# Both products of the attention scores over 128 partitions: the low parts of the keys kept twice

## The chip, the core and the metric

The kernel runs as one launch on one core of a Trainium2 chip. The metric is the device time of that launch in microseconds (us). A difference between two kernels is read from repeated runs of both.

## The reference, cut to what matters

Two blocks follow each other, on 1024 tokens of 1024 channels, in float32. The first block holds a gated branch and an attention with 16 heads of 64 channels; the second a state-space layer, an embedding, an attention with 16 heads of 64 channels again ("stick-breaking"), and another embedding. The change concerns the scores of the two attentions alone, the products of queries with keys:

```python
# first block, dilated_pattern
s = jnp.einsum('bhrnqd,bhrnkd->bhrnqk', qb, kw) * (Dh ** -0.5)
...
# second block, stick_breaking_mixer, for each block of 128 queries
z = jnp.einsum('bhtd,bhsd->bhts', q[:, :, q0:kend], k[:, :, :kend]).astype(jnp.float32)
```

The kernel computes the first block's three dilated patterns as one causal attention over all earlier keys, with a table that is added to the scores. So both attentions have the same shape: for each head, eight tiles of 128 queries, each against all keys up to its own end.

## The kernel before, in words

Products run on TensorE (PE) in a rounded float32 type. To keep precision, an operand is held as a high part (the rounded value) and a low part (the rest), and a product is a sum of products of parts.

**Order.** A planner written in Python gives out the instructions: streams (generators) yield what they wait for, and the ready stream with the best priority goes on, judged by rough costs of each instruction. So the order in which each engine's instructions stand is fixed when the program is built, and a changed dependency or an added instruction changes that order from there on. On the chip each engine runs its list in order and waits on semaphores.

**Attention.** `attention1` (first block) and `stick` (second block) both work through eight pairs of heads. For a pair, `project_pair` makes four dense products (values, queries, keys, a gate), each 2 halves of 512 tokens times 24 matmuls of 128 rows and 512 columns. Between these, the streams of the scores, of the transposes of the weights and of the products with the values put in their own matmuls.

**Stacks.** The 64 channels of a head fill half of the 128 partitions, so `stacks_q` puts the high part of a head's queries on its own half and the low part on the other half. `stacks_k` writes the high part of the keys on both halves (ACT, four copies for each half of the tokens) and the low parts of both heads of the pair into one third tile, each on its own half (DVE, two subtractions, `lo_part`). The pools are cut in `stack_pools`: the tiles named m108r hold queries and high parts of the keys, m140r the low parts.

**Scores.** `scores` makes one tile of 128 queries against up to 512 keys with two matmuls that add into one bank of PSUM: the first contracts all 128 partitions (high and low queries against the high keys), the second contracts the 64 partitions of the head (high queries against the low keys). A head needs 12 such pairs of matmuls: 2 of 128 columns, 2 of 256, 2 of 384 and 6 of 512. For 16 heads and 2 attentions that makes 384 pairs.

**After the scores.** In `attention1` DVE adds the table and takes the maximum, ACT exponentiates, DVE normalises. In `stick` DVE adds a mask, ACT takes two sigmoids, DVE runs a scan (L2017) and POOL a multiplication. Then, in both, PE transposes the weights (L527), ACT and DVE split them (m156r), PE multiplies them with the values into a single bank of PSUM (`pv`), and ACT and DVE take the sum out (m192f).

Of the kernel before, what the change touches and what calls it, by code (L numbers as in the profile page):

```python
# [28 lines left out]
KB4 = 1024  # float32 elements in 4 KB  # L29
# [7 lines left out]
def at(scale, part):  # L37
    """a factor, or the part of a column of factors"""
    return scale if isinstance(scale, float) else scale[part, :]


class Tok:
    """estimated time at which something is ready; None until it is issued"""
# [5 lines left out]
class Bank:  # L49
    """a slot of PSUM"""  # L50
# [12 lines left out]
class Block:  # L63
    """a part of the arena that holds values of one kind at a time: "f" float32, "r" rounded for float32r products"""
# [5 lines left out]
class Arena:  # L70
    """storage of 4-byte values; off and n are in KB a partition"""

    CUTS = (0, 8, 16, 24, 40, 44, 60, 76, 92, 108, 140, 156, 172, 192, 200)
# [41 lines left out]
class Region:  # L115
    """a part of the arena; free when no overlapping region is held"""
# [25 lines left out]
class Ring:  # L142
    """storage given out in turn, sizes in KB"""
# [4 lines left out]
    def next(self, n):  # L148
        """region to be waited for and taken by the caller, in the order of the calls"""
        if self.pos + n > self.n:  # L150
            self.pos = 0
        r = self.b.region(self.off + self.pos, n)
        self.pos += n
        return r


class Res:
    """slots of storage, any of which will do"""
# [24 lines left out]
class Some:  # L183
    """n slots at once"""
# [10 lines left out]
class At(float):  # L195
    """time at which an engine is done with something"""
# [12 lines left out]
def seen(t, eng):  # L209
    """when engine eng can act on what is done at t"""  # L210
    own = getattr(t, "eng", None)
    return float(t) if own is None else t + (OWN[eng] if own == eng else LAT)
# [20 lines left out]
class Idle:  # L233
    """an engine without work given out ahead"""
# [9 lines left out]
class Sched:  # L244
    """Order of issue. Streams (generators) give instructions out and yield what their next ones wait for; the ready
    stream of the best priority goes on, judged by rough costs of the instructions given out so far."""
# [43 lines left out]
    def pe(self, ns, rows=P):  # L290
        """the clock of the tensor engine is halved in the tick after one with too little work"""
# [11 lines left out]
class Act:  # L303
    """activations, channels on partitions, split: quadrants [kh][th] of [128, 2 (hi, lo), 4 channel tiles, 512 tokens]"""
# [17 lines left out]
    def part(self, j, kh, t):  # L322
        """[128, 4, 128]: channel tiles of half kh, token tile t"""
        return self.quad(kh, t // 4)[:, j, :, (t % 4) * P:(t % 4) * P + P]

    def row(self, j, k, th):
        """[128, 512]: channel tile k, token half th"""
# [10 lines left out]
class Job:  # L338
    """one product; its weights are read in blocks [(granule, ...), ...] in the order of use"""

    def __init__(self, b, w, c0, ncols, kind, kt=KT, k0=0, gain=None, more=None):
        """more = (c, n): n columns from c on go with the last block"""
# [16 lines left out]
class Weights:  # L359
    """float32 blocks of up to 1024 values a partition, read ahead and split in the order in which they were added"""  # L360
# [53 lines left out]
    def limit(self, n, m=2):  # L414
        """use the first n split blocks and m unsplit ones only"""
# [6 lines left out]
class Builder:  # L422
# [28 lines left out]
    def banks(self, *names):  # L451
        """the banks to be used from now on for products, transposes, the rest of a phase, and sums"""
# [3 lines left out]
    def at(self, off, n):  # L456
        """n KB at off KB of the arena"""
        return self.arena.at(off, n)
# [72 lines left out]
    def evacuate(self, bank, r):  # L531
        """r: the time of the last read of the bank, or a stream that ends with it"""
# [9 lines left out]
    def gemm_b(self, act, job, evac, begin=None, each=None, free=None):  # L542
        """out[c, t] = sum_k w[k, c] x[t, k]; evac(cb, half, psum [128, 512], time) gives the time of its last read;
        free(half) when nothing reads that half of act any more"""
# [9 lines left out]
    def half_b(self, act, job, cb, half, evac, each):  # L554
        """gemm_b's product of one block and one half of the tokens"""
# [14 lines left out]
    def freed(self, act):  # L570
        """tokens of the times from which on nothing reads a half of act, and the function that sets them"""
# [9 lines left out]
    def gemm_a(self, act, job, evac, fin=None, k0=0, begin=None, late=()):  # L581
        """out[t, c]; evac(cb, tile, psum [128, 256], time), after begin(cb, tile); in the first block the tiles in late have banks of their own
        in which they wait for the last channels together"""
# [49 lines left out]
    def rstd(self, src, n, junk, dep, eps=EPS):  # L633
        """(mean of squares + eps) ** -0.5 of each row; stream"""
# [10 lines left out]
    def to_act(self, act, src, t, dep):  # L645
        """transposes of token tile t ([128 tokens, channels]) into act; stream"""
# [19 lines left out]
    def raw_tile(self, act, src, t, dep, nj, half):  # L666
        """act's token tile t = src, transposed; half[t] = half the factor of its norm; stream"""
# [12 lines left out]
    def norm_tile(self, act, src, t, g, dep, nj, done=None):  # L680
        """act's token tile t = rmsnorm(src) * g, transposed; stream"""
# [13 lines left out]
    def bcast(self, dst, row):  # L695
        """row [1, n] on every partition"""
        return self.dma(dst, row.to_broadcast([P, row.shape[1]]))

    def load_cols(self):
        """columns of channels in self.col; filled by the stream given back"""  # L700
# [36 lines left out]
    def plan(self):  # L737
        """products in the order in which they run, so that their weights can be read ahead"""
# [52 lines left out]
    def main(self):  # L791
        """the products, in order; everything else runs beside them"""
# [21 lines left out]
    def norm_in(self):  # L814
# [16 lines left out]
        def tile_(t):  # L831
            # the weights' first blocks come after the first tile
# [11 lines left out]
    def branch_a(self):  # L844
# [14 lines left out]
        def prep():  # L859
            # needed by the mixing only  # L860
# [75 lines left out]
    def spill(self, slots, kind, dst, toks, c0=0):  # L936
        """evac and each of channel-major products that go to DRAM; kind "silu2": 2 silu(x), "sig": tanh(x / 2) = 2 sigmoid(x) - 1"""
# [25 lines left out]
    def taken(self, region, blocks=0):  # L963
        """token of the time at which the region has become ours"""
# [12 lines left out]
    def load_act(self, act, rows, slots, mul=None, go=None):  # L977
        """streams: act's channel tiles from DRAM rows [(source, token)]; with mul: half the product with it"""
# [33 lines left out]
    def gates_a(self):  # L1012
        self.banks("01", "23", "456", "7")
        """silu of the attention gate to DRAM"""
# [6 lines left out]
    def merge(self):  # L1021
        self.banks("012", "3", "456", "7")
        """gate a * (ya @ w_proj_a) + gate b * (yb @ w_proj_b), split in act2; its product with w_out, two norms"""
# [4 lines left out]
        # the last gate fills the tail of the attention  # L1028
# [79 lines left out]
    def gated(self, act, job, gate, gtok, gl, out, dst, dtok):  # L1108
        """(gate + 1) * product to DRAM"""
# [27 lines left out]
    UNITS = [(h, g) for h in range(2) for g in (0, 1, 3, 2)]  # L1137

    def stack_pools(self):
        self.qsr, self.khr = self.res(108, 4, 4, "r"), self.res(124, 4, 4, "r")  # L1140
        self.klr, self.vsr = self.res(140, 4, 2, "r"), self.res(148, 8, 2, "r")

    def stacks_q(self, st, half, src, scale, e):
        """st = (head 0, head 1): own half of the partitions the high part, the other half the low part; stream"""
# [15 lines left out]
    def stacks_k(self, st, half, src, scale, e):  # L1160
        """st = (high parts of head 0 twice, of head 1 twice, low parts of both); stream"""
# [6 lines left out]
        for h, (own, oth) in enumerate(HALVES):  # L1168
            yield (e, s.FV)
            e = self.lo_part(st[2][own, tk], src[own, :], at(scale, own), st[h][own, tk], e)  # L1170
        return e

    def v_tile(self, vT, half, vs, e, done):
        """token-major stacks (high | low and low | high columns) of a pair from vT [128, 512]; stream"""
# [1065 lines left out]
```

## Time and profile before

| | before |
|---|---|
| median of 3 runs | 3373.07 us (3372.86 to 3374.96) |
| span of the profiled execution | 3370.6 us |
| instructions in it | 47748 |
| PE busy | 3229.0 us (96%) |
| DVE busy | 1680.2 us (50%) |
| ACT busy | 1364.6 us (40%) |
| POOL busy | 1257.3 us (37%) |

The span runs from the first to the last instruction of one profiled execution; some 2.5 us of the median lie outside it. Times in views are us from the start of the span, if not marked ns. Matmuls are pipelined: a row's duration runs to the modelled end of the matmul, and the next one can start before it. What a matmul costs its engine is therefore read as the distance from its start to the start of the next. "64\*128 64x512" means weights of 64 rows by 128 columns, and 64 rows by 512 columns that stream past them.

### The profile page before, as it was taken

The numbers are of one execution on the slowest core, as the hardware profiler recorded it, in microseconds if no ns is written. First come the engines' busy times: TensorE is split into PE (matmuls) and PEld (weight loads), VectorE is DVE, ScalarE is ACT, GpSimd is POOL, SyncE is SP. The second block draws the span as 40 slices with busy tenths as digits, with TensorE's granted clock in tenths as the row PEclk, the third lists the DMA queues.
The fourth block names the chain that finished last, engine by engine and source line by source line (L and its number), as shares of the span: only waits on it lengthen the run. The fifth ranks groups of instructions, "written<-read, shape, count | busy, mean of one in ns | idle before, by whom it ended". The sixth has DMA issues, their size and how long they took to land.

```text
span 3370.6 us, 47748 instructions
## 1 busy us (share of the span) xinstructions
PE 3229.0 (96%) x18830; PEld 2743.8 (81%) x18830; DVE 1680.2 (50%) x3080; ACT 1364.6 (40%) x2505; POOL 1257.3 (37%) x772
## 2 busy tenths in 40 slices
PE   8999999999999999988989889999999999998999
PEld 8888877777778889976868788899977777776899
DVE  2111156666664321556565564443457667677552
ACT  4322245545554311433232323213456556665421
POOL 3332111111112433234444444543335455557760
PEclk9999999999999999999999989999999999998999
DMA  4122211111112843323333334451201111112531
GB/s 133 51 76 78 78 62 58 52 51 51 57 55 85 274 157 137 102 72 73 107 79 105 80 107 124 144 198 38 82 22 38 38 37 35 36 38 93 189 118 51
DMA packets 296053, 291.35 MB, mean 86 GB/s; under 512 B 15556, under 2 KB 252276, under 8 KB 295828
## 3 DMA queue, kind: packets, MB, share of 16 engines
q1 hardware_dynamic: 295828, 288.29, 27.4%
q8 instruction: 148, 2.42, 0.3%
q14 instruction: 77, 0.63, 0.1%
HBM read 216.80 MB, written 71.43 MB: 86 GB/s over the span
## 4 chain that ended last, share of the span: by engine, by line
PE 82%; DVE 7%; DMA 6%; issue 2%; POOL 2%; ACT 1%; SPq 0%; POOLq 0%; ACTq 0%; DVEq 0%
PE psum L516 75%; PE psum L527 6%; DMA m92f<-acum 3%; DVE m24f L2017 2%; DMA m172f<-acum 1%; DVE m76f L493 1%; POOL m172f L501 1%; DVE m92f L489 1%; DVE m156r L482 1%; DVE m60f L493 0%; DMA m172f<-zd 0%; DVE m192f L482 0%; DVE m44f L493 0%; DMA m172f<-yd 0%; DVE m108r L493 0%
## 5 line engine op out<-in xcount | busy, mean ns | idle before, releaser
L501 POOL TENSOR_TENSOR m8r<-m0f,m8r 128x1024 fp32r<-128x1024 f32 (+1 forms) x67 | 169.4, 2529 | 538.1 <-ACT m8r L478 516.9
L501 POOL TENSOR_TENSOR m16r<-m0f,m16r 128x1024 fp32r<-128x1024 f32 x64 | 158.8, 2481 | 411.9 <-ACT m16r L478 406.4
L482 DVE TENSOR_TENSOR m156r<-psum,m156r 128x384 fp32r<-128x384 f32 (+2 forms) x376 | 221.6, 605 | 126.2 <-ACT m156r L478 125.0
L478 ACT ACTIVATE m156r<-psum 128x384 fp32r<-128x384 f32 (+2 forms) x376 | 194.0, 532 | 202.7 <-PE psum L527 196.4
L501 POOL TENSOR_TENSOR m24r<-m0f,m24r 128x1024 fp32r<-128x1024 f32 (+1 forms) x67 | 163.0, 2437 | 266.7 <-ACT m24r L478 263.6
L501 POOL TENSOR_TENSOR m172f<-m172f,m24f 128x127 f32<-128x127 f32 (+7 forms) x128 | 180.1, 1416 | 179.1 <-DVE m24f L2017 126.0
L2017 DVE TENSOR_TENSOR_SCAN m24f<-m24f,zero 128x128 f32<-128x128 f32 (+7 forms) x128 | 230.7, 1812 | 10.2 <-ACT m24f L478 9.5
L478 ACT ACTIVATE m192f<-psum 64x256 f32<-64x256 f32 (+2 forms) x240 | 105.0, 437 | 273.2 <-PE psum L516 194.8
L527 PE MATMUL psum<-ident,m172f 128*128 128x128 f32 (+1 forms) x1314 | 202.7, 278 | 10.7 <-POOL m172f L501 4.3
L493 DVE SCALAR_TENSOR_TENSOR m172f<-m172f,psum 128x256 f32<-128x256 f32 (+1 forms) x112 | 59.9, 534 | 279.8 <-ACT m172f L478 216.4
L516 PE MATMUL psum<-m140r,m108r 64*128 64x512 f32 (+3 forms) x384 | 170.7, 445 | 1.0 <-DVE m140r L493 1.0
L527 PEld LDWEIGHTS psum<-ident,m172f 128*128 128x128 f32 (+1 forms) x1314 | 149.5, 142 | 24.8 <-POOL m172f L501 5.2
L501 POOL TENSOR_TENSOR smalls<-smalls,mhalf 128x1 f32<-128x1 f32 (+1 forms) x104 | 83.4, 805 | 212.2 <-DVE smalls L489 202.5
L1410 ACT ACTIVATE m172f<-m172f,smalls 128x128 f32<-128x128 f32 (+7 forms) x128 | 99.1, 775 | 151.6 <-DVE smalls L489 151.5
L516 PE MATMUL psum<-m108r 128*128 128x512 f32 (+3 forms) x384 | 151.4, 394 | 3.9 <-ACT m172f L478 3.4
L1402 DVE CUSTOM_DVE_ANT_0 m172f<-psum,m24f 128x512 f32<-128x512 f32 (+1 forms) x192 | 106.6, 556 | 84.1 <-PE psum L516 81.0
L516 PEld LDWEIGHTS psum<-m140r,m108r 64*128 64x128 f32 x384 | 71.0, 185 | 93.7 <-issue 85.2
L501 POOL TENSOR_TENSOR m0f<-m0f,cols 128x1024 f32<-128x1024 f32 x64 | 129.1, 2018 | 27.8 <-PE psum L516 10.0
L478 ACT ACTIVATE m40f<-psum 128x256 f32<-128x256 f32 (+1 forms) x149 | 65.7, 444 | 177.7 <-PE psum L516 136.0
L516 PE MATMUL psum<-m60r,m8r 128*128 128x512 f32 x492 | 132.6, 402 | 0.0
L516 PE MATMUL psum<-m44r,m8r 128*128 128x512 f32 x492 | 131.7, 403 | 0.2 <-DVE m108r L493 0.2
L516 PE MATMUL psum<-m92r,m16r 128*128 128x512 f32 x480 | 131.0, 406 | 0.0
(361 smaller groups left out, 7991.9 us busy)
## 6 DMA issues: line engine op xcount, KB each, us to landing
m0f<-in_w_in_dram SPq DMA_DIRECT2D x72, 512.0 KB, 3.6
m0f<-in_m_in_dram SPq DMA_DIRECT2D x38, 512.0 KB, 4.5
m92f<-acum SPq DMA_DIRECT2D x21, 512.0 KB, 8.6
m24f<-in_alibi_dram SPq DMA_DIRECT2D x16, 512.0 KB
zd<-m40f SPq DMA_DIRECT2D x64, 128.0 KB, 1.9
m172f<-zd SPq DMA_DIRECT2D x32, 256.0 KB, 9.0
yd<-m172f SPq DMA_DIRECT2D x32, 256.0 KB, 2.2
m0f<-in_m_out_dram SPq DMA_DIRECT2D x16, 512.0 KB, 3.8
```

What stands on the lines that cost most here:

```text
L478: self.nc.scalar.activation(out, in_, func, **k)
L482: self.nc.vector.tensor_tensor(out, a, b, op=op)
L489: self.nc.vector.tensor_scalar(out, a, s1, s2, op0=op0, op1=op1)
L493: self.nc.vector.scalar_tensor_tensor(out, a, s, b, op0=op0, op1=op1)
L501: self.nc.gpsimd.tensor_tensor(out, a, b, op=op)
L516: self.nc.tensor.matmul(out, l, r, start=start, stop=stop)
L527: self.nc.tensor.transpose(out, in_, self.ident[:in_.shape[0], :in_.shape[0]])
L1402: nc.vector.tensor_tensor_reduce(row[:, k0:k0 + w], bank[:, :w], Tt[:, off + k0:off + k0 + w], 1.0, -3e38, op0=ALU.add, op1=ALU.max, accum ...
L1410: nc.scalar.activation(row[:, :n], row[:, :n], AF.Exp, bias=nm, accum_out=l)
L2017: nc.vector.tensor_tensor_scan(x[:, ::-1], x[:, ::-1], self.zero.to_broadcast([P, n]), 1.0, op0=ALU.mult, op1=ALU.add)
```

## The change

The low parts of each head's keys get a tile of their own, with the low part on both halves of the partitions. `stacks_k` writes the low part on the head's own half as before (DVE) and then ACT copies it to the other half. The second matmul of `scores` contracts all 128 partitions, so that it now also adds low queries times low keys. There are four tiles of low parts in place of two, the new ones in a new block of 16 KB at 200 KB (named m200r), and the builder is asked for a smaller area of DMA descriptors, which makes room for it. The changed file has no comments and docstrings either.

```diff
-    CUTS = (0, 8, 16, 24, 40, 44, 60, 76, 92, 108, 140, 156, 172, 192, 200)
+    CUTS = (0, 8, 16, 24, 40, 44, 60, 76, 92, 108, 140, 156, 172, 192, 200, 216)
...
-        self.klr, self.vsr = self.res(140, 4, 2, "r"), self.res(148, 8, 2, "r")
+        self.klr = Res([self.region(o, 4, "r") for o in (140, 144, 200, 204)])
+        self.vsr = self.res(148, 8, 2, "r")
...
         for h, (own, oth) in enumerate(HALVES):
             yield (e, s.FV)
-            e = self.lo_part(st[2][own, tk], src[own, :], at(scale, own), st[h][own, tk], e)
-        return e
+            lo = self.lo_part(st[2 + h][own, tk], src[own, :], at(scale, own), st[h][own, tk], e)
+            yield (lo, s.FA)
+            e2 = self.A(R(st[2 + h][oth, tk]), st[2 + h][own, tk], AF.Copy, lo)
+        return max(lo, e2)
...
-            yield from into("k", self.khr, self.khr, self.klr)
+            yield from into("k", self.khr, self.khr, self.klr, self.klr)
...
-        for x, r in zip(o["q"] + o["k"], (self.qsr, self.qsr, self.khr, self.khr, self.klr)):
+        for x, r in zip(o["q"] + o["k"], (self.qsr, self.qsr, self.khr, self.khr, self.klr, self.klr)):
...
     def scores(self, ps, o, h, i, k0, w):
-        own = HALVES[h][0]
         tk = slice(i * P, i * P + P)
         self.mm(ps, R(o["q"][h][:, tk]), R(o["k"][h][:, k0:k0 + w]), True, False)
-        return self.mm(ps, R(o["q"][h][own, tk]), R(o["k"][2][own, k0:k0 + w]), False, True)
+        return self.mm(ps, R(o["q"][h][:, tk]), R(o["k"][2 + h][:, k0:k0 + w]), False, True)
...
-    nc = _bacc.Bacc("TRN2", target_bir_lowering=False, num_devices=1)
+    nc = _bacc.Bacc("TRN2", dynamic_dma_scratch_size=1024, target_bir_lowering=False, num_devices=1)
```

The program has the same instructions on PE, DVE, POOL and the DMA queue as before, and 64 more on ACT. Their order differs from the first scores on. On PE, where `attention1` starts the scores of its first pair of heads, before the change (a row's shape is that of the result, so that the rows of the contraction don't show; m140r marks the second product; m92r and m44r are the dense product):

```order
L516 MATMUL psum<-m92r,m8r 128x512 x9
L516 MATMUL psum<-m108r 128x128
L516 MATMUL psum<-m140r,m108r 128x128
L516 MATMUL psum<-m108r 128x256
L516 MATMUL psum<-m140r,m108r 128x256
L516 MATMUL psum<-m92r,m8r 128x512 x3
L516 MATMUL psum<-m108r 128x384
L516 MATMUL psum<-m140r,m108r 128x384
```

The same place after the change:

```order
L516 MATMUL psum<-m92r,m8r 128x512 x12
L516 MATMUL psum<-m108r 128x128
L516 MATMUL psum<-m200r,m108r 128x128
L516 MATMUL psum<-m108r 128x256
L516 MATMUL psum<-m200r,m108r 128x256
L516 MATMUL psum<-m44r,m16r 128x512 x3
L516 MATMUL psum<-m108r 128x384
L516 MATMUL psum<-m200r,m108r 128x384
```

The two products stand in the same alternation; the second reads the new tile, and the scores moved behind three more matmuls of the dense product.

On ACT, where the same pair's stacks are made, before the change (m108r rows write queries and high keys, m24r, m16r and m8r rows are splits of weights, L1410 is the exponential):

```order
L478 ACTIVATE m108r<-psum 64x512 x4
L1410 ACT_TABLE_LOAD
L1410 ACTIVATE m172f,smalls<-m172f,smalls 128x128
L1410 ACTIVATE m172f,smalls<-m172f,smalls 128x256
L478 ACTIVATE m8r<-m0f 128x1024
L478 ACTIVATE m108r<-psum 64x512
```

The same place after the change (the exponential is L1412 there):

```order
L478 ACTIVATE m108r<-psum 64x512 x4
L478 ACTIVATE m200r<-m200r 64x512 x2
L478 ACTIVATE m8r<-m0f 128x1024
L478 ACTIVATE m108r<-psum 64x512
L1412 ACT_TABLE_LOAD
L1412 ACTIVATE m172f,smalls<-m172f,smalls 128x128
```

The two copies stand behind the high parts, and ahead of a split of weights and of the first exponential.

On ACT in `stick`, a pair of heads in the middle of the stage after the change (before, no row of m200r stood there; m24f and m172f are the two sigmoids, m40f a projection on its way out):

```order
L478 ACTIVATE m108r<-psum,smalls 64x512
L478 ACTIVATE m200r<-m200r 64x512
L478 ACTIVATE m40f<-psum 128x512
L478 ACTIVATE m200r<-m200r 64x512
L478 ACTIVATE m108r<-psum,smalls 64x512
L478 ACTIVATE m24f<-psum,rq 128x128
```

Each copy stands in the middle of ACT's list and waits there for its subtraction on DVE.

## Rows read from the trace of the kernel before

**Rows 1.** Page: span, then the chain that ended last, by engine.

```profile
span 3370.6 us, 47748 instructions
PE 82%; DVE 7%; DMA 6%; issue 2%; POOL 2%; ACT 1%; SPq 0%; POOLq 0%; ACTq 0%; DVEq 0%
```

**Rows 2.** Windows, by stage: most of attention1, most of stick, the state-space layer.

```profile
core 0: us, PE busy (x) PEld busy (x) DVE busy (x) ACT busy (x) POOL busy (x), PEclk, DMA share, GB/s
435.00:1080.00 645.00, 644.78 (x3206) 495.86 (x3205) 395.45 (x1076) 325.67 (x662) 79.31 (x33) 1.00 0.18 54
2480.00:3170.00 690.00, 652.99 (x3339) 503.80 (x3337) 494.27 (x680) 435.34 (x837) 406.61 (x243) 0.98 0.16 48
1400.00:2250.00 850.00, 765.02 (x4772) 677.65 (x4771) 459.81 (x763) 263.29 (x456) 374.24 (x248) 0.94 0.38 109
```

**Rows 3.** Timeline, PE, in attention1: start, length, engine, line, operation.

```profile
511.18 2.90 PE L516 MATMUL psum<-m60r,m8r 128*128 128x512 f32 x12
513.92 2.20 PE L516 MATMUL psum<-m92r,m8r 128*128 128x512 f32 x9
515.96 0.22 PE L516 MATMUL psum<-m108r 128*128 128x128 f32 x1
516.11 0.33 PE L516 MATMUL psum<-m140r,m108r 64*128 64x128 f32 x1
516.36 0.38 PE L516 MATMUL psum<-m108r 128*128 128x256 f32 x1
516.68 0.38 PE L516 MATMUL psum<-m140r,m108r 64*128 64x256 f32 x1
516.99 0.96 PE L516 MATMUL psum<-m92r,m8r 128*128 128x512 f32 x3
517.79 0.34 PE L516 MATMUL psum<-m108r 128*128 128x384 f32 x1
518.05 0.44 PE L516 MATMUL psum<-m140r,m108r 64*128 64x384 f32 x1
518.42 0.50 PE L516 MATMUL psum<-m108r 128*128 128x512 f32 x1
518.85 0.49 PE L516 MATMUL psum<-m140r,m108r 64*128 64x512 f32 x1
519.27 0.96 PE L516 MATMUL psum<-m44r,m16r 128*128 128x512 f32 x3
```

**Rows 4.** Timeline, weight loads (PEld) at the same place; idle in brackets.

```profile
513.69 2.00 PEld L516 LDWEIGHTS psum<-m92r,m8r 128*128 128x128 f32 x9
515.73 0.19 PEld L516 LDWEIGHTS psum<-m108r 128*128 128x128 f32 x1
516.11 0.18 PEld L516 LDWEIGHTS psum<-m140r,m108r 64*128 64x128 f32 x1 [0.18 <-issue]
518.85 0.18 PEld L516 LDWEIGHTS psum<-m140r,m108r 64*128 64x128 f32 x1 [0.24 <-issue]
```

**Rows 5.** Windows of m108r on PE (all score matmuls): attention1, stick.

```profile
435.00:1080.00 645.00, 139.73 (x384) 1.00 0.18 54
2480.00:3170.00 690.00, 147.47 (x384) 0.98 0.16 48
```

**Rows 6.** Lines by shape: ACT and DVE rows of the stacks, attention1 then stick.

```profile
L478 ACT ACTIVATE m108r<-psum 64x512 fp32r<-64x512 f32 x92 | 54.3, 590 | 12.0 <-PE psum L516 10.7
...
L2017 DVE TENSOR_TENSOR_SCAN m24f<-m24f,zero 128x1024 f32<-128x1024 f32 x16 | 42.8, 2677 | 0.0
...
L493 DVE SCALAR_TENSOR_TENSOR m140r<-psum,smalls,m108r 64x512 fp32r<-64x512 f32 x32 | 23.9, 747 | 6.4 <-ACT m108r L478 5.9
...
L478 ACT ACTIVATE m108r<-psum,smalls 64x512 fp32r<-64x512 f32 x96 | 65.4, 681 | 23.6 <-PE psum L527 22.1
```

**Rows 7.** Waits of PE in stick, 2400 to 3170: total, times, longest.

```profile
PE psum L516 <- DVE m156r L482: 16.3, 11, 4.5
PE psum L516 <- DVE m192f L482: 8.0, 7, 1.8
```

## The prediction, made before the changed kernel ran

> **What bounds the kernel now.** I read the chain that ended last first: PE makes 82% of it [rows 1]. The question is then how far each attention stage hangs on PE, so the windows by stage come next [rows 2]. In attention1 PE is busy 644.78 of 645 us, with DVE at 61%, ACT at 50% and POOL at 12%; the granted clock is 1.00, its upper level (2.4 GHz). This stage is as long as PE's list. In stick PE is busy 652.99 of 690 us and idle for 37.0; DVE is at 72%, ACT at 63%, POOL at 59%. PE leads there too, but others sometimes stop it: the longest totals are waits for the split of the weights (16.3 us) and for the bank of the sums (8.0), both of DVE [rows 7].
>
> Busy time doesn't say what a matmul costs, so I went to single starts in attention1 [rows 3]. Twelve dense matmuls of 512 columns go from 511.18 to 513.92: 2.74 / 12 = 0.228 us each, 0.445 ns a column. At that rate two matmuls would take 0.114 us for 128 columns, 0.228 for 256, 0.342 for 384 and 0.456 for 512. The pairs of the scores, from the start of the first product to whatever follows the second, take: 128 columns, 515.96 to 516.36, 0.40; 256 columns, 516.36 to 516.99, 0.63; 384 columns, 517.79 to 518.42, 0.63; 512 columns, 518.42 to 519.27, 0.85. The excess is 0.29, 0.40, 0.29 and 0.39 us. It doesn't grow with the columns: it comes in two sizes, about 0.29 where the pair follows dense matmuls and about 0.40 where it follows another pair. So it is no streaming time, but a fixed price of going into a matmul of 64 rows and out again.
>
> The weight loads show how [rows 4]. For a dense matmul the load stands some 0.23 us ahead (515.73, for the matmul of 515.96). For the 64-row matmul of 516.11 it starts with it, at 516.11, after 0.18 us of idle time that nothing explains; at 518.85 after 0.24. The load isn't taken ahead when the number of rows changes.
>
> **Part 1: the second product goes from 64 to 128 rows.** No count changes: 384 pairs, 192 in each attention. If the excess goes, a pair saves 0.29 to 0.40 us, so 384 pairs save 111 to 154. A second way narrows that: PE is busy with score matmuls for 139.73 us in attention1 and 147.47 in stick [rows 5]. This counts a modelled end beyond the next start in each pair, about 0.07 us (518.85 + 0.49 against 519.27), 13 us a stage: 126 and 134 are left. Dense, 192 pairs of 384 columns on average would take 192 x 0.342 = 66. So 60 and 68 us could go, 128 in all; from both ways I take 64 in attention1 and 66 in stick, 130 together.
>
> Is it the 64 rows, rather than something else in the pair? Two products into one bank, and twice the same weights, also stand in every dense product (the code multiplies the high weights with the high and then the low activations), at 0.228 us [rows 3]. What is left that only these matmuls have is their 64 rows.
>
> **Part 2: 64 more copies on ACT.** Four for each pair of heads (two heads by two halves of the tokens), 16 pairs: 64. No row shows a copy of 64x512 from SBUF to SBUF; the nearest are the same shape from PSUM, 590 ns without and 681 with a column of factors [rows 6]. The copies have no such column, so 0.59: 19 us a stage; bounds 0 and 0.68 (22 us). They lie beside PE: ACT is idle for 319 us of attention1 and 255 of stick. Uncovered, all of them would cost 38 us.
>
> A copy waits for its subtraction on DVE, and ACT's list waits behind it: splits of weights, exponentials or sigmoids, copies of transposes, all of which PE needs. In attention1 DVE is at 61% and the first pair's copies stand ahead of the first exponential; PE has the next pair's dense products to go on with. I take nothing there but 2 us for the first pair, whose scores also moved behind three dense matmuls that had to run anyway. In stick a subtraction can stand behind a scan of up to 2.68 us [rows 6]; that goes into part 3.
>
> **Part 3: what others give back.** In attention1 the saved 64 us shorten 645 to 581; DVE would be at 68%, ACT at 59% with its copies. PE never had to wait there, so I take 62. In stick, 690 less 66 is 624 us, and DVE's 494 would be 79% of it, ACT's 435 + 19 73%, POOL's 407 65%. DVE's list is in order and has long scans, and its waits stopped PE already at 72%. Bounds: nothing given back (66 saved), or all of it. By the distance of DVE's 494 to 624 the stage still has room, so I stay near the first: PE's idle time grows by half, from 37 to 55, and 18 us are given back; 48 saved.
>
> **Part 4: nothing else.** The new block overlaps no other. DMA is at 16 to 18% in these stages [rows 2]; the smaller area of descriptors I cost at nothing, since no DMA is added and the transfers have that room. The order outside the attentions is nearly that of before, but in stick it is shuffled; the range carries that, with some 10 us either way.
>
> **Sum.** 3370.6 - 62 - 48 = 3260.6 us of span. The profiled span lies 2.5 us under the median of the runs, so the time is 3263 us, 110 less than 3373 (3.3%).
>
> **The rivals.**
>
> *All of it arrives.* PE sets the pace in stick too and its waits stay at 37 us. For it: DVE would have 21% of idle time left. Against it: every one of PE's waits in stick is for an engine that has in-order work behind PE's own. 3373 - 130 = 3243; with a better shuffle 3235. Chance 17%.
>
> *Stick keeps its length.* DVE, with the scans and the transposes' splits in one list, becomes the pace there, or the granted clock falls when PE waits more: in the state-space layer, where PE is busy 90%, it is 0.94 on average [rows 2]. Time at the lower of two levels is then 12%, and the same in stick's 624 us would lose 37. Then attention1's 62 us and 0 to 20 of stick's: 3291 to 3311. Chance 11%.
>
> *The rows don't matter.* If the excess belonged to the pair (its switch of operands, say) and not to the 64 rows, PE's list would be as long as before, the copies would be hidden, and the time would stay at 3373, with 5 us either way. Against it: dense matmuls switch operands too, at 0.228. Chance 5%. The Trainium skill has a rule on that side, in "TensorE: Matmul & The Clock Gate", Why this matters for your kernels: a single matmul with few contracted rows takes as long as one with 128. By that rule alone the change would save nothing; the trace agrees for the streaming and differs for what lies around it. Another page, "TensorEngine Tiling (Array Packing)", says under Key Properties that changing the tiling mode, which a contraction of 64 rows is there, drains TensorE; by that one the sum is the 130 us of part 1, and the excess that doesn't grow with the columns agrees.
>
> *Slower: ACT stands behind DVE.* Each copy holds ACT until its subtraction is done. If a scan stands ahead of it, ACT waits for up to 2.68 us, then copies for 0.59, and PE runs out of split weights and transposes. If PE felt all of that, the 32 copies in stick would cost 32 x 3.27 = 105 us; at 1.5 us (DVE's two subtractions of 0.75 [rows 6]) and 0.59 the 32 in attention1 cost 67: 172 against the 130 gained, 3415 us. It decides from 130 / 64 = 2.0 us that PE loses for each copy. Against it: in attention1 PE waits for nobody, and both engines are idle for a third of their time. Chance 3%.
>
> **How the numbers follow.** The forecast of 3263 holds 64%, with its own range of 3246 to 3288 (a give-back in stick between 0 and 38 us, with the shuffle). The range of 8 in 10 takes in most of the first rival and half of the second: 3235 to 3302; out are some 4% below, 5% of the second rival, and the last two with 8%. This kernel's time can be told from no change from about 0.2% (7 us) on. Faster: 64 + 17 + 11%, and 1% of the third: 93%. The same: 4%. Slower: 3%.
>
> **What would show it.** Right: in the timeline a pair of 512 columns takes 0.46 us, at any place, with its weight load some 0.2 us ahead; a pair of heads in attention1, with 24 score pairs, takes 8 us less, and PE stays at 99%; ACT has 64 more rows of 0.6 us. In stick PE's idle time is between 37 and 75 us. Wrong: pairs still at 0.63 to 0.85; PE waiting for the tiles of the keys; copies on ACT with long waits for DVE ahead of them; a granted clock below 0.95 in stick.

## The result, and the profile after

The changed kernel takes 3293.79 us (median of 4 runs, 3290.80 to 3296.86) against 3374.02 for the kernel before (4 runs): 80 us less, a ratio of 0.9761 with a 95% interval of 0.9748 to 0.9773. The forecast was 3263, in a range of 3235 to 3302. The gain is 80 us where 110 were forecast. The time lies in the wide range, but 6 us above the forecast's own range (3246 to 3288), among the times of the rival in which stick keeps its length (3291 to 3311).

The page of the kernel after, span and chain, against [rows 1]:

```profile
span 3295.1 us, 47821 instructions
PE 76%; DVE 12%; DMA 6%; issue 2%; ACT 2%; POOL 2%; SPq 0%; DVEq 0%; POOLq 0%; ACTq 0%
```

DVE's share of the chain rose from 7 to 12%. The windows of the kernel after, by stage (most of attention1, most of stick, the state-space layer), against [rows 2]:

```profile
435.00:1015.00 580.00, 577.37 (x3224) 497.08 (x3223) 381.19 (x1077) 348.54 (x697) 79.21 (x33) 1.00 0.20 61
2418.00:3089.00 671.00, 596.42 (x3295) 504.87 (x3294) 489.88 (x676) 449.47 (x862) 408.92 (x241) 0.96 0.16 49
1333.00:2185.00 852.00, 770.56 (x4771) 682.81 (x4770) 457.93 (x763) 263.07 (x455) 373.44 (x248) 0.94 0.38 109
```

The second column is PE. In attention1 it is still busy 577 of 580 us. In stick it is busy 57 us less than before, but idle for 74.6 us instead of 37.0, and its granted clock is 0.96 on average instead of 0.98. So about 38 of the 57 us have turned into waiting. The two windows of stick don't hold quite the same work (3339 and 3295 rows on PE), so this is rough; rows64 below gives two stretches with the same work.

The timeline of the kernel after on PE, in attention1, against [rows 3]:

```profile
523.30 0.40 PE L516 MATMUL psum<-m108r 128*128 128x512 f32 x1
523.54 0.39 PE L516 MATMUL psum<-m140r,m108r 128*128 128x512 f32 x1
523.77 0.34 PE L516 MATMUL psum<-m108r 128*128 128x384 f32 x1
523.94 0.34 PE L516 MATMUL psum<-m140r,m108r 128*128 128x384 f32 x1
524.12 0.86 PE L516 MATMUL psum<-m92r,m16r 128*128 128x512 f32 x3
524.82 0.40 PE L516 MATMUL psum<-m108r 128*128 128x512 f32 x1
```

A pair of 512 columns takes 523.77 - 523.30 = 0.47 us and one of 384 takes 0.35, where 0.85 and 0.63 stood before: nearly the rate of the dense matmuls. The three dense matmuls behind the pair take 0.70 us (524.12 to 524.82), nearly their own rate (0.68) too; behind a pair in [rows 3] three of them took 0.80 (516.99 to 517.79). The weight loads of the same stretch, against [rows 4]:

```profile
523.30 0.19 PEld L516 LDWEIGHTS psum<-m140r,m108r 128*128 128x128 f32 x1
523.54 0.19 PEld L516 LDWEIGHTS psum<-m108r 128*128 128x128 f32 x1
```

The load for the matmul of 523.54 starts at 523.30, 0.24 us ahead of it, with no idle time noted. The windows of all score matmuls on PE, attention1 and then stick, against [rows 5], say the same in total:

```profile
437.40:1017.40 580.00, 92.61 (x384) 1.00 0.20 62
2421.00:3089.00 668.00, 101.43 (x384) 0.96 0.17 49
```

In attention1 139.73 became 92.61. A dense pair's modelled end lies 0.16 us beyond the next start (523.54 + 0.39 against 523.77), 31 us for 192 pairs, so 62 are left, against 126 before: about 64 us gone by the same rough way as in part 1 of the prediction. It leaves out the 0.10 us that the row behind a pair gained.

The copies, by shape, in attention1 and then in stick; the last number is the idle time of ACT before them:

```profile
L478 ACT ACTIVATE m200r<-m200r 64x512 fp32r<-64x512 f32 x16 | 10.1, 631 | 3.6 <-DVE m200r L482 3.0
L478 ACT ACTIVATE m140r<-m140r 64x512 fp32r<-64x512 f32 x16 | 10.1, 630 | 4.8 <-DVE m140r L493 4.5
```

One takes 0.63 us (0.59 was taken), and ACT stands idle for 0.2 to 0.3 us before it. The waits of PE in stick, total, times and longest, against [rows 7]:

```profile
PE psum L516 <- DVE m156r L482: 33.4, 26, 3.0
PE psum L516 <- DVE m192f L482: 13.7, 11, 2.2
PE psum L527 <- POOL m172f L501: 10.3, 8, 3.5
PE psum L527 <- DVE m140r L482: 9.0, 7, 3.2
```

The two waits for DVE that led before have grown from 16.3 to 33.4 and from 8.0 to 13.7 us. One of them, in a timeline of the kernel after, PE first and then ACT, DVE and POOL:

```profile
2761.85 0.28 PE L516 MATMUL psum<-m156r 128*128 128x256 f32 x1
2765.02 0.90 PE L516 MATMUL psum<-m156r 128*128 128x256 f32 x3 [2.89 <-DVE m156r L482]
2765.72 0.73 PE L516 MATMUL psum<-m108r 128*128 128x512 f32 x1
2766.26 0.63 PE L516 MATMUL psum<-m200r,m108r 128*128 128x512 f32 x1
...
2759.42 0.49 ACT L478 ACTIVATE m156r<-psum 128x384 fp32r<-128x384 f32 x1
...
2759.41 1.50 DVE L493 SCALAR_TENSOR_TENSOR m200r<-psum,smalls,m108r 64x512 fp32r<-64x512 f32 x2
2760.94 3.44 DVE L2019 TENSOR_TENSOR_SCAN m24f<-m24f,zero 128x512 f32<-128x512 f32 x1
2764.41 0.56 DVE L482 TENSOR_TENSOR m156r<-psum,m156r 128x384 fp32r<-128x384 f32 x1
...
2760.94 2.36 POOL L501 TENSOR_TENSOR m16r<-m0f,m16r 128x1024 fp32r<-128x1024 f32 x1 [0.44 <-ACT m16r L478]
```

ACT has the high part of the transposed weights ready at 2759.91. DVE's list has two subtractions of keys and a scan ahead of the low part, which is ready at 2764.97 only; PE waits for 2.89 us. The two matmuls of 512 columns after the wait start 0.54 us apart, where 0.23 is the rate at the upper level of the clock: from 2765 to 2768 the granted clock is 0.50, its lower level (1.2 GHz). Such places lower the stage's mean to 0.96.

### The profile page after: what moved, and what is told of

Read it like the earlier page. It is cut to its first block, busy times and chain, and to the rows that moved or that the text cites. A ratio compares the mean times of both kernels' runs of the same rounds, so it can differ in the third digit from the quotient of the medians.

```text
span 3295.1 us, 47821 instructions
## 1 busy us (share of the span) xinstructions
PE 3115.5 (95%) x18830; PEld 2755.9 (84%) x18830; DVE 1669.9 (51%) x3080; ACT 1402.5 (43%) x2569; POOL 1262.6 (38%) x772
## 4 chain that ended last, share of the span: by engine, by line
PE 76%; DVE 12%; DMA 6%; issue 2%; ACT 2%; POOL 2%; SPq 0%; DVEq 0%; POOLq 0%; ACTq 0%
PE psum L516 70%; PE psum L527 6%; DVE m24f L2019 4%; DMA m92f<-acum 3%; DMA m172f<-acum 1%; DVE m156r L482 1%; DVE m76f L493 1%; DVE m92f L489 1%; DVE m172f L1404 1%; POOL m172f L501 1%; DVE m60f L493 0%; ACT m108r L478 0%; DVE m172f L487 0%; DVE m192f L482 0%; DVE m108r L493 0%
## 5 line engine op out<-in xcount | busy, mean ns | idle before, releaser
L501 POOL TENSOR_TENSOR m172f<-m172f,m24f 128x127 f32<-128x127 f32 (+7 forms) x128 | 188.5, 1484 | 156.0 <-DVE m24f L2019 105.4
L501 POOL TENSOR_TENSOR m24r<-m0f,m24r 128x1024 fp32r<-128x1024 f32 x65 | 158.0, 2432 | 221.7 <-ACT m24r L478 220.4
L2019 DVE TENSOR_TENSOR_SCAN m24f<-m24f,zero 128x128 f32<-128x128 f32 (+7 forms) x128 | 233.5, 1831 | 8.5 <-ACT m24f L478 8.0
L516 PE MATMUL psum<-m108r 128*128 128x512 f32 (+3 forms) x384 | 141.4, 371 | 5.3 <-ACT m172f L478 3.5
L1412 ACT ACTIVATE m172f<-m172f,smalls 128x128 f32<-128x128 f32 (+7 forms) x128 | 99.3, 776 | 95.5 <-DVE smalls L489 94.4
L516 PE MATMUL psum<-m76r,m16r 128*128 128x512 f32 x504 | 132.6, 398 | 0.0
L516 PE MATMUL psum<-m76r,m8r 128*128 128x512 f32 x492 | 131.3, 401 | 0.0
L516 PE MATMUL psum<-m44r,m16r 128*128 128x512 f32 x504 | 130.4, 396 | 0.0
```

The costliest lines, as they stand in the source:

```text
L501: self.nc.gpsimd.tensor_tensor(out, a, b, op=op)
L516: self.nc.tensor.matmul(out, l, r, start=start, stop=stop)
L1412: nc.scalar.activation(row[:, :n], row[:, :n], AF.Exp, bias=nm, accum_out=l)
L2019: nc.vector.tensor_tensor_scan(x[:, ::-1], x[:, ::-1], self.zero.to_broadcast([P, n]), 1.0, op0=ALU.mult, op1=ALU.add)
```

## The experiments

All medians are of 4 or 5 runs (one run for the last two), beside 7 or 8 of the kernel before on the same chip, at 3373.4 to 3374.4 us.

**rows64: the contraction alone taken back.** Tiles, copies and nearly the order of the changed kernel stay (18656 of PE's 18830 places hold the same matmul of the same tiles):

```diff
-        return self.mm(ps, R(o["q"][h][:, tk]), R(o["k"][2 + h][:, k0:k0 + w]), False, True)
+        own = HALVES[h][0]
+        return self.mm(ps, R(o["q"][h][own, tk]), R(o["k"][2 + h][own, k0:k0 + w]), False, True)
```

> The changed kernel, with its copies, its tiles and nearly its order on every engine, but the second product of the scores contracts the 64 partitions of the head again; the low queries times low keys are left out, as before the change. If the fixed price belongs to the 64 rows, the pairs take 0.40 to 0.85 us again by their columns, and the time is 3374 us or somewhat more (up to 3385, since the copies and the order stay): the whole gain is gone. If the gain came from the new tiles or the new order, the time stays near 3294. If the copies on ACT hold up PE, this kernel is slower than the one before the change by what they cost.

3386.3 us (3384.13 to 3390.76), ratio to the kernel before 1.0039 (1.0025 to 1.0054): the whole gain is gone, and the time is 1 us over the most that was expected. In its timeline the pairs have their old lengths:

```profile
519.94 0.34 PE L516 MATMUL psum<-m108r 128*128 128x384 f32 x1
520.21 0.44 PE L516 MATMUL psum<-m140r,m108r 64*128 64x384 f32 x1
520.57 0.50 PE L516 MATMUL psum<-m108r 128*128 128x512 f32 x1
521.00 0.49 PE L516 MATMUL psum<-m140r,m108r 64*128 64x512 f32 x1
521.43 2.35 PE L516 MATMUL psum<-m44r,m16r 128*128 128x512 f32 x9
```

0.63 us for 384 columns and 0.86 for 512. So the 64 rows alone are worth 3386 - 3294 = 92 us in this order, and all the rest of the change, order and copies, costs 12.

The two kernels also tell what each stage gets, without a shuffle between them. Attention1 goes from 615.6 us in rows64 (first to last second product, 438.5 to 1054.1) to 549.4 in the changed kernel (438.5 to 987.9): 66 us less. Stick, from its first score matmul to its last, in rows64 and then in the changed kernel, in the columns of the windows above:

```profile
2487.50:3161.90 674.40, 640.55 (x3185) 488.03 (x3183) 465.06 (x661) 442.54 (x845) 374.83 (x233) 0.97 0.15 44
2421.60:3071.60 650.00, 579.74 (x3181) 489.56 (x3180) 477.16 (x660) 440.18 (x843) 392.20 (x232) 0.96 0.15 45
```

Stick gets only 24 us shorter: PE is busy 61 us less, but idle for 70.3 us instead of 33.9.

**only_first and only_stick: the change in one attention.** A flag for the stage decides on the copy and on the rows of the second product:

```diff
+            e2 = lo
+            if self.twice:
+                yield (lo, s.FA)
+                e2 = self.A(R(st[2 + h][oth, tk]), st[2 + h][own, tk], AF.Copy, lo)
...
+        rows = slice(0, 128) if self.twice else HALVES[h][0]
+        return self.mm(ps, R(o["q"][h][rows, tk]), R(o["k"][2 + h][rows, k0:k0 + w]), False, True)
```

> The change in attention1 alone; stick contracts 64 rows in the second product and makes no copies. The markers of the two profiles put 67 us of the gain before the state-space layer. Theory (PE sets the pace in attention1, and the price goes in full): 3305 to 3312 us. If the gain of attention1 were given back in the stages behind it, which have work of their own, 3320 or more.

> The change in stick alone; attention1 contracts 64 rows in the second product and makes no copies. The markers of the two profiles leave 10 to 20 us for stick. Theory (DVE's list stops PE there): 3354 to 3364 us, with PE idle for 65 to 80 us of the stage. If the small gain in stick comes from what attention1's change does to the order behind it, stick alone gives its 48 us or more: 3326 or less.

only_first: 3307.64 us, 66.5 less than before (0.9803, 0.9789 to 0.9818). only_stick: 3350.94, 23 less (0.993, 0.9915 to 0.9945), 3 us under what was expected; PE is idle there for 62.8 us from the first score matmul of stick to the last, where 65 to 80 were expected. Attention1's gain stayed to the end; stick gave 23 alone, and 80 - 66.5 = 14 beside attention1's. So the shortfall against the forecast is in stick, and it is there without attention1's change.

**order_noise: the same instructions, shuffled.**

```diff
-LAT = 180.0
+LAT = 200.0
```

> The changed kernel with one constant of the planner, the delay that it assumes between two engines, at 200 in place of 180. No instruction is added or taken away; the order is shuffled. It measures what a shuffle alone is worth. If the order explains the 30 us by which the forecast was off, this time lies elsewhere by 15 us or more; if DVE's work explains them, it stays within 10 us of 3294.

3300.2 us (3297.42 to 3303.14), 6 more than the changed kernel. By the total alone, within 10 us, the order would not matter. But the total hides shifts: the last second product of attention1 starts at 1000.0, 12 us later than in the changed kernel (987.9), and later stages make half of it good. PE is idle for 11 us of attention1 there (568.91 of 580 us busy), so even that stage is free of waits only under some orders. A shuffle moves a stage by ten or more, so the order can't be left out of the account of stick.

**noscan_before and noscan_after: both kernels without the scans of stick.** Their order stays, since the planner still counts the scan:

```diff
-            nc.vector.tensor_tensor_scan(x[:, ::-1], x[:, ::-1], self.zero.to_broadcast([P, n]), 1.0,
-                                         op0=ALU.mult, op1=ALU.add)
```

> The kernel before the change without the scans of stick: the instruction is left out, the planner still counts its cost, and the order on every engine stays as it was. DVE has some 230 us less to do in stick. Theory: PE's 37 us of idle time in the stage mostly go, 3335 to 3355 us. It is to be held against the changed kernel without the scans.

> The changed kernel without the scans of stick, its order as it was. Theory (DVE's list of scans and splits stops PE in stick, and eats what the shorter score pairs save): without the scans the gain of the change comes in full, 115 to 135 us between this and the kernel before without the scans, so 3210 to 3235. Rival (the copies, which hold ACT until DVE's subtraction is done, or the shuffled order): the gap stays near 80 us, so 3255 to 3275.

3326.85 us (3321.25 to 3329.44) and 3197.08 us (3192.56 to 3200.35). Both are faster than was expected, by 8 and 13 us; their difference lies where the theory put it. The change is worth 129.8 us between these two, where it is worth 80 with the scans. (The two differ in order too, as the kernels before and after do.) Stick in noscan_after, in the columns of the windows above:

```profile
2418.00:2975.00 557.00, 548.74 (x3182) 478.05 (x3181) 268.15 (x535) 434.51 (x840) 334.55 (x232) 0.98 0.18 53
```

PE is idle for 8 us (4 of 625 in noscan_before), ACT does all its copies, and the order is that of the changed kernel. So neither the copies nor the order by itself eats the gain; it takes the scans on DVE. Leaving them out also shortens POOL's work (334.55 us, 408.92 in the changed kernel), so this run alone doesn't tell DVE's list from POOL's; the waits of PE do, which name DVE for most of the time.

**few_copies: 48 of the 64 copies left out.** The planner still counts them:

```diff
+        self.ncopy = 0
...
-            e2 = self.A(R(st[2 + h][oth, tk]), st[2 + h][own, tk], AF.Copy, lo)
+            if self.ncopy % 32 < 8:
+                e2 = self.A(R(st[2 + h][oth, tk]), st[2 + h][own, tk], AF.Copy, lo)
+            else:
+                e2 = s.op("A", 95 + 0.833 * 512, lo)
+            self.ncopy += 1
```

> The changed kernel with the copies of the first two pairs of heads in each attention alone; the later 48 are left out, so that the second product reads what those wrote on the other half, and the planner still counts them. Rival (the copies hold up ACT's list, and it PE): 20 to 35 us faster than the changed kernel, 3260 to 3275. Theory (they lie in ACT's idle time): within 10 us, 3284 to 3296.

3289.52 us (3284.53 to 3290.86), 4 less than the changed kernel. Where the rival of ACT behind DVE expected 20 to 35, 48 of 64 copies are worth 4 us at most: they are nearly all covered, and this rival is out.

**scan_cost, scan_cost_before, scan_cost_more: another plan.** The planner counted 75 + 1.042 ns a column for a scan: 0.61 us for 512 columns. In stick of the changed kernel one takes 2.02 on average:

```profile
L2019 DVE TENSOR_TENSOR_SCAN m24f<-m24f,zero 128x512 f32<-128x512 f32 x16 | 32.4, 2024 | 0.2
```

All 128 scans take 233.5 us by its page, and the plan has 86 for them. The same instructions are planned for a slower scan, in the changed kernel and in the one before (239 us for all), and slower still with 1000 + 2.6 ns a column (320 us):

```diff
-            e = s.op("V", 75 + 1.042 * n, e)
+            e = s.op("V", 600 + 2.2 * n, e)
```

> The changed kernel with another cost of the scan in the planner: 600 + 2.2 ns for each column, as its rows in the profile have it, in place of 75 + 1.042. The instructions are the same, their order in stick is planned for the slower scan. If PE waits because the plan has DVE done sooner than it is, part of the 30 us comes back: 3265 to 3285. If DVE's work itself is the pace, or the order doesn't matter, the time stays within 7 us of 3294.

> The kernel before the change with the planner's cost of the scan at 600 + 2.2 ns for each column. It tells whether the 53 us that this cost gave the changed kernel belong to the change. If the wrong cost only hurts where PE is fast enough to meet DVE's lag, this kernel gains little, as PE has 37 us of idle time in stick at most: 3340 to 3374, and the change is then worth 100 to 130 us under the better plan. If the cost is worth the same 53 us here, 3315 to 3327, the change is still worth only 80.

> The changed kernel with the planner's cost of the scan still higher, 1000 + 2.6 ns for each column. If what is left in stick (PE idle by some 40 us) is still the plan's lead over DVE: 3220 to 3235. If the plan has reached what the order can give: 3235 to 3250.

scan_cost: 3240.59 us (3236.05 to 3249.67), 53 less than the changed kernel and 0.9609 of the kernel before (0.9589 to 0.963): the fastest version with all of the work. scan_cost_before: 3345.43 us (3343.10 to 3348.91), 29 less than before, as the theory had it. scan_cost_more: 3272.78 us. The first is faster than was expected (3265 to 3285), the third slower than either theory had it (3220 to 3250). Stick in scan_cost, in the columns of the windows above, and its waits of PE:

```profile
2418.00:3013.00 595.00, 558.13 (x3157) 478.57 (x3156) 476.63 (x656) 436.71 (x840) 395.91 (x231) 0.98 0.17 49
```

```profile
PE psum L516 <- DVE m156r L482: 11.0, 12, 2.5
PE psum L527 <- POOL m172f L501: 9.3, 4, 4.7
PE psum L516 <- DVE m192f L482: 4.7, 4, 3.3
```

PE is idle for 36.9 us of this stretch, half of the 74.6 of the changed kernel. DVE has the same scans to do and is busy 80% of the stretch, where it was 73%. So its load as such is not the bound; the order of the lists, with the places of the long scans in DVE's, is worth these 38 us. But the kernel before waits less under this plan too:

```profile
2480.00:3129.00 649.00, 639.92 (x3308) 497.78 (x3306) 466.31 (x667) 428.77 (x827) 384.17 (x235) 0.98 0.16 48
```

PE is idle for 9.1 us there, where it was 37.0. So the shorter pairs still bring some 28 us of waiting under this plan, and the change is worth 3345 - 3241 = 105 us. The third version shows that a higher cost isn't better, by 32 us. The best of the three plans is the one whose total fits the measured scans (239 against 233.5 us); with three points, in a program where a shuffle alone moves the time, that is a hint and not shown.

**low_twice_64 and low_twice_128: what a second matmul of 64 rows costs.** The second product is issued twice, in the kernel before (below) and, with all rows and its own tile, in the changed one:

```diff
+        self.mm(ps, R(o["q"][h][own, tk]), R(o["k"][2][own, k0:k0 + w]), False, False)
         return self.mm(ps, R(o["q"][h][own, tk]), R(o["k"][2][own, k0:k0 + w]), False, True)
```

> The kernel before the change with the second product of each score tile issued twice, so that high queries times low keys count double. Two matmuls of 64 rows then follow each other. If the fixed price is for changing the number of rows, the added matmul costs its columns alone, 0.06 to 0.23 us, and attention1 grows by 192 x 0.171 = 33 us. If each matmul of 64 rows pays about 0.2 us on its own, the distance of the two is 0.25 to 0.43 us and the stage grows by 71.

> The changed kernel with the second product of each score tile issued twice, with 128 rows. For both theories the added matmul costs its columns alone, and attention1 grows by 33 us against the changed kernel. It is the measure that low_twice_64 is held against: a plan with the added product in it, at a price that isn't disputed.

From the first to the last second product, attention1 grew from 617.4 us (436.0 to 1053.4) to 656.8 (435.5 to 1092.3) with 64 rows, 39 us; with 128 from 549.4 (438.5 to 987.9) to 580.1 (438.0 to 1018.1), 31. In total, 3447.55 and 3335.74 us. The timeline of low_twice_64 in attention1:

```profile
522.82 0.62 PE L516 MATMUL psum<-m140r,m108r 64*128 64x384 f32 x2
523.37 0.50 PE L516 MATMUL psum<-m108r 128*128 128x512 f32 x1
523.79 0.73 PE L516 MATMUL psum<-m140r,m108r 64*128 64x512 f32 x2
524.46 3.02 PE L516 MATMUL psum<-m44r,m16r 128*128 128x512 f32 x12
```

Two matmuls of 64 rows and 512 columns hold PE for 0.67 us, where one held it for 0.42: the second adds 0.25, its columns at the dense rate are 0.23. So the price isn't paid by each matmul of 64 rows (that would have been 71 us); nearly all of it is paid once for going there and back. Each of the two is one run, and a shuffle moved attention1 by 12 us, so 39 and 31 are rough; the single starts say the same.

## Why the prediction came out as it did

**The price of the 64 rows: right in kind, misread in size.** The excess is gone where the second product has 128 rows (0.47 and 0.35 us a pair), and back in rows64, which has nearly the same order. It is paid for a change of rows, not by each matmul of 64 rows (low_twice_64). But its two sizes, 0.29 behind dense matmuls and 0.40 behind another pair, are one. Where dense matmuls follow the pair, some 0.12 us of the price falls on them (0.80 for three in [rows 3], for 0.68), and where a pair follows, on that pair's first product, which made the second pair look dearer. So each visit costs about 0.40 us, 77 for an attention and 154 for both, by the rates of [rows 3]; part 1's second way, by the busy time of the score matmuls alone, could not see what falls on the row behind. That 129.8 us arrive without the scans, where 130 were forecast, is in part luck: two orders stand between those two kernels, and order and copies cost 12 us in rows64.

**Attention1: right.** 62 us were forecast; 66 arrive in the same order, and 66.5 alone. Of the 77 us by the rows some 11 are missing, a few of them new waits (PE is idle for 2.6 us of the window, before for 0.2), and a few the pairs' own, at 0.01 us each over the dense rate; for the rest no row gives a reason. The 2 us for the first pair's late start stand in the profile (438.5 against 436.0 for the first second product).

**The copies and the order.** The copies were right: 0.63 us each for 0.59, 4 us of time for 48 of them. Copies and order together cost 12 us in rows64, where the sum had 2, and 10 either way in its range.

**What stick gives back: the term that was mis-sized.** Part 3 let PE's idle time in stick grow by half, from 37 to 55 us, gave 18 us back, and took 48 for the stage. In nearly the same order, rows64 against the changed kernel, the idle time doubles, from 33.9 to 70.3 us, and the stage gives 24. Against attention1's 66 that is 42 us given back: 36 as idle time, and about 6 by the lower clock (an estimate: 4% of 650 us lost, against 3% of 674). The mechanism was named, DVE's list in order with long scans, and noscan shows that it takes the scans. The size was taken from DVE's load, "the stage still has room", and load alone was the wrong measure: with the same scans and DVE busier, at 80%, scan_cost has half the idle time. What counts is whether PE needs something that stands behind a scan, as in the wait of 2.89 us above. A likely reason that the kernel before met this less, argued and not shown: the plan has 86 us for scans that take 233.5, so DVE runs late against it, and the planner has no price for a change of rows, so PE ran late too, by 8 to 10 us for every pair of heads (24 visits of 0.35 to 0.40 us), until the change took that away.

**The sum.** 80 us are 66 in attention1 and 26 in stick and behind it, both at one order, less 12 for the order and the copies; the forecast had 62 and 48. So of the missing 30 us, 22 are stick's and 12 the order's and the copies', and attention1 gave 4 more than was forecast. The time is one that the second rival forecast (3291 to 3311, chance 11%), with its 0 to 20 us from stick. Of its two reasons, DVE as the pace is not it, as scan_cost does the same scans in a stage some 55 us shorter (595 against 650 us); the clock did fall, from 0.98 to 0.96, where the rival had 0.94.

**What stays open.** How much of the give-back a better order can save isn't settled. Orders of the same instructions lie between 3241 and 3300 us (scan_cost, scan_cost_more, the changed kernel, order_noise). Under the two plans tried in both kernels the change is worth 80 and 105 us, and PE's idle time in stick still grows from 9 to 37 us under the better one. The time of scan_cost, 3240.59, is near what the first rival forecast for a stick that gives all (3243), but its plan also gives the kernel before 29 us.

The two rules of the Trainium skill weighed in the prediction came out so: "TensorEngine Tiling (Array Packing)", Key Properties, with its drain at a change of the tiling mode, agrees with the price that is paid once for each visit (0.67 us for two matmuls of 64 rows and 512 columns, 0.42 for one). "TensorE: Matmul & The Clock Gate", Why this matters for your kernels, which has few rows take as long as 128, fits the second of two matmuls of 64 rows (0.25 us for 512 columns, 0.23 dense) and does not hold here, where 64 rows stand among 128 and rows64 is 92 us slower.

## What to carry to other kernels

Read what a matmul costs from start to start, and hold it against a dense one: an excess that doesn't grow with the columns is a price of the neighbourhood, here of a change in the number of contracted rows, and filling up the rows removes it, though it adds products that nobody asked for. Read on to the matmul behind it, since a part of the price can fall there. When the engine that leads gets faster, most of its gain arrives where nothing else ever stopped it; where the profile shows waits, ask which long instruction stands ahead of what it waits for, and not only how busy that engine is. In a kernel with a planner, hold the planner's costs against the durations in the profile before and after such a change. To price a change that also changes the order, make a version that keeps the new order and takes the change alone back.

## What the runs showed of the hardware that was not expected

A scan of the same shape has very different lengths: 512 columns took 3.44 us at 2760.94 in the changed kernel, while POOL ran a subtraction of 2.36 us that started at the same instant. In other places of the same profile it runs without POOL's work beside it, and short:

```profile
2753.63 0.42 DVE L2019 TENSOR_TENSOR_SCAN m24f<-m24f,zero 128x128 f32<-128x128 f32 x1 [1.10 <-ACT m24f L478]
2755.36 0.68 DVE L2019 TENSOR_TENSOR_SCAN m24f<-m24f,zero 128x256 f32<-128x256 f32 x1
```

These two give 0.42 us for 128 columns and 0.26 for each further 128, so about 1.2 for 512 (an estimate from these rows). A row of the kernel before, with no work of POOL beside it, bears that out:

```profile
2688.93 1.21 DVE L2017 TENSOR_TENSOR_SCAN m24f<-m24f,zero 128x512 f32<-128x512 f32 x1
```

1.21 + 2.36 = 3.57 is near the 3.44. The scans lengthen POOL's work too: in noscan_after its rows in stick take 334.55 us (232 of them) against 408.92 (241) in the changed kernel. The Trainium skill has a rule for this in "SBUF — State Buffer", Terms: DVE and GpSimd arbitrate for a shared pair of ports, and the loser waits for the whole instruction. These numbers agree with it, though no run took POOL's work away.

Going from matmuls of 128 rows to one of 64 and back costs about 0.40 us, whatever the columns and the neighbours, and it is spread over three places. In [rows 3] the first product of a pair behind dense matmuls takes some 0.1 us more than its columns (515.96 to 516.11 for 128 columns, 0.06 dense), the second some 0.2 (516.11 to 516.36), and the three dense matmuls behind the next pair 0.12 together (516.99 to 517.79). The weight loads fit: a load of 64 rows starts with its matmul and not ahead of it [rows 4].
